# Norm sums and one row of b multiplied as rounded part plus rest in fp32r, and the first weight row issued from ScalarE's queue, in a two-layer decoder trunk on one core

## The chip, the core and the metric

The kernel runs on one core of one Trainium2 chip. The metric is device time in microseconds (us) of one execution; lower is better. Engines are named as the profile names them: PE (TensorE matmuls), PEld (its weight loads), DVE (VectorE), ACT (ScalarE), POOL (GpSimd) and SP (SyncE, which issues most DMAs).

## What is computed

One sequence of 256 tokens with 2048 channels goes through two layers. Layer 0 is a pooling mixer and a gated convolutional feed-forward network (FFN, width 5504); layer 1 is an attention with dilated windows and another such FFN. After each of the four parts comes a residual sum and a layer norm. All is float32.

```
for i in range(DEPTH):                      # DEPTH = 2
    mix = pool_mixer(h, ...) if i == 0 else dilated_attention(h, k_shared, v_shared, ...)
    h = layer_norm(ALPHA * h + mix, ln1_g[i], ln1_b[i])
    ff = conv_ffn(h, ffn_w_up[i], ffn_conv_w[i], ffn_conv_b[i], ffn_w_down[i])
    h = layer_norm(ALPHA * h + ff, ln2_g[i], ln2_b[i])

def layer_norm(x, g, b):
    mu = mean(x); var = mean((x - mu) ** 2)
    return (x - mu) * rsqrt(var + 1e-5) * g + b
```

## The kernel before

Activations lie channel-major: tile `H[q]` holds 4 blocks of 128 channels by 256 tokens. Every weight matrix is cut into units of 512 rows by up to 512 columns, over 360 of them, which run in one fixed list. `run_units` (the driver) takes them in order: it issues the loads of units up to `LD_AHEAD` = 5 ahead (`do_load`, L69, on SP's queue), splits the weights of units up to 3 ahead, runs the unit's matmuls on PE, and then runs small jobs that were put off with `later(n, fn)`.

The matrix products are made in fp32r, a rounded float32 format that PE multiplies in one pass. To keep precision each operand is split into a rounded part and the rest: `do_split` casts the weights on ACT (`wh`, L86) and subtracts on DVE (`wl`, L87). A product then takes three matmuls (L181 and L183, or L185 to L187).

Three of the four norms go through `chain`. By then DVE has summed the values and the squares of the 16 channel blocks into `ST["S"]` and `ST["Q"]`, 128x256 each. `chain` sums them over the 128 partitions with two plain fp32 matmuls against `invd`, a matrix of 1/2048 (L396, L397; the trace has two instructions for each). Then ACT squares the mean (L402), DVE subtracts (L403), ACT takes the root (L404), DVE the reciprocal (L405). The driver puts this job behind the last matmul of a unit; the split of the weights of three units on stands ahead of it on ACT and DVE.

The last norm works on tokens as rows. Once the first 128 tokens are complete `finish_first` normalises them (L729 on ACT; L686 times g and L735 plus b on DVE) while PE makes the rest of the last products. `finish_second` does the other 128 tokens with matmuls against diagonal matrices: L748, L753, L754 (`ident` times a row of b) and L758, and L762 on DVE makes the outputs, which L689 stores.

At the start SP issues the pieces of x and the rows of the first weight unit by turns; PE transposes x (L524); ACT, and for one half DVE, copies the result to `XC` (L530, L528), and the first products (L172) follow.

The order on every engine is that of the code: each engine takes its instructions in order. The pool `lnp` has one buffer for each tag, so a new tile of a tag waits until the last reader of the one before is done. The tag `fold2` is used by the folds, by `var` and by a small diagonal at the end; the tag `sq` by the squares, by `rm` and by `w3`.

Of the kernel before, what the change touches and what calls it, by code (L numbers as in the profile page):

```python
# [9 lines left out]
F32 = mybir.dt.float32  # L10
F32R = mybir.dt.float32r
I32 = mybir.dt.int32
AF = mybir.ActivationFunctionType
OP = mybir.AluOpType
# [3 lines left out]
T = 256  # L18
P = 128
# [14 lines left out]
def trunk(ctx: ExitStack, tc: tile.TileContext, x, pool_w_in, pool_w_grp, pool_scale, pool_w_out,  # L34
# [26 lines left out]
    def do_load(i, part=None):  # L61
        src = units[i][0]
        nk, n = src.shape[0] // P, src.shape[1]
        if not part:
            raw[i] = rawp.tile([P, nk, n], F32, name=f"raw{i}", tag="raw")
        rows = src.rearrange("(k p) n -> p k n", p=P)
        ks = pieces(i, nk)
        for s in ks if part is None else ks[2:] if part else ks[:2]:
            nc.sync.dma_start(raw[i][:, s], rows[:, s])  # L69

    parts = {}

# [201 lines left out]
    ident = const.tile([P, P], F32, name="ident")  # L274
    invd = const.tile([P, P], F32, name="invd")
    ones4 = const.tile([P, P], F32R, name="ones4")
    epst = const.tile([P, 1], F32, name="epst")
    inv = const.tile([P, 1, 16], F32, name="inv")
    cnt = const.tile([P, 3, P], F32, name="cnt")
# [113 lines left out]

    def chain(ps, lay, which, after):
        mean, msq = ps[:, :T], ps[:, T:]
        PE.matmul(mean, invd, ST["S"], start=True, stop=True)  # L396
        PE.matmul(msq, invd, ST["Q"], start=True, stop=True)  # L397
        t2 = lnp.tile([P, 2, T], F32, name="var", tag="fold2")
        rm = lnp.tile([P, 4, T], F32, name="rm", tag="sq")[:, 0:2]
        rs, mr = rm[:, 0:1, :], rm[:, 1:2, :]  # L400
        ST["rs"], ST["mr"] = rm[:, 0, :], rm[:, 1, :]
        A.activation(t2[:, 0, :], mean, AF.Square)  # L402
        V.tensor_tensor(t2[:, 1, :], msq, t2[:, 0, :], OP.subtract)  # L403
        A.activation(t2[:, 1, :], t2[:, 1, :], AF.Sqrt, bias=epst)  # L404
        V.reciprocal(rm[:, 0, :], t2[:, 1, :])  # L405
        V.tensor_tensor(rm[:, 1, :], mean, rm[:, 0, :], OP.mult)
        mb, rb = mr.to_broadcast([P, 4, T]), rs.to_broadcast([P, 4, T])
        g0 = 32 * which

        def spread():  # L410
            for i in range(4):
                PE.matmul(ps[:, i * P:i * P + P], one1, dg[:, i, :], start=True, stop=True)
            A.copy(rm.rearrange("p a t -> p (a t)"), ps)
            norm(0)

        def norm(q):
            V.tensor_tensor(H[q], H[q], rb, OP.mult)
            V.tensor_tensor(H[q], H[q], mb, OP.subtract)

        def affine(q):  # L420
            XC[q] = quad_tile("xc")
            for m in range(4):
                j = 4 * q + m
                A.activation(H[q][:, m, :], H[q][:, m, :], AF.Identity,
                             scale=vec[lay][:, g0 + j:g0 + j + 1], bias=vec[lay][:, g0 + 16 + j:g0 + 17 + j])
            A.copy(XC[q][:, :, 0, :T], H[q])

        def lo(q):
            lo_part(XC[q], H[q], 4)
            if after is not None:  # L430
                later((13, 16, 20, 22)[q], lambda: after(q))

        later(1, lambda: norm(0))
        for q in range(4):
            later(2 + q, lambda q=q: affine(q))
            if q < 3:
                later(2 + q, lambda q=q: norm(q + 1))
            later(3 + q, lambda q=q: lo(q))
# [75 lines left out]
    def x_quad(q, halves=(0, 1)):  # L514
        xin = XIN
        if halves[0] == 0:
            H[q] = hp.tile([P, 4, T], F32, name="h", tag="h")
            XC[q] = quad_tile("xc")
        for half in halves:
            ps = bank("xT")  # L520
            for kk in range(2):
                for t in range(2):
                    k = 2 * half + kk
                    PE.transpose(ps[:, kk * T + t * P:kk * T + t * P + P], xin[q, t][:, k * P:(k + 1) * P], ident)  # L524
            pv2 = ps.rearrange("p (k t) -> p k t", k=2)
            s = slice(2 * half, 2 * half + 2)
            if q == 0 and half == 1:
                V.tensor_copy(XC[q][:, s, 0, :T], pv2)  # L528
            else:
                A.copy(XC[q][:, s, 0, :T], pv2)  # L530
            V.tensor_tensor(XC[q][:, s, 1, :T], pv2, XC[q][:, s, 0, :T].bitcast(F32), OP.subtract)
            before.setdefault(min(q + 1, 3), []).append(lambda s=s, pv2=pv2: A.copy(H[q][:, s, :], pv2))
# [158 lines left out]
    def tm_post(c, first, last):  # L691
# [33 lines left out]
        def finish_first():  # L725
            rs, mr = scales(moments(0))
            for cc in range(4):
                z = HT[cc][:, 0, :]
                A.activation(z, z, AF.Identity, scale=rs, bias=mr)  # L729
            for cc in range(2):  # L730
                times_g(cc, 1)
            for cc in range(4):
                z = HT[cc][:, 0, :]
                times_g(cc, 0)
                V.tensor_tensor(z, z, ST["b"][:, cc, :], OP.add)  # L735
                store(cc, 0)

        def finish_second():
            def y(cc):
                return HT[cc][:, 1, :]  # L740

            def diag(nm, tag):
                return lnp.tile([P, P], F32, name=nm, tag=tag)

            g, b = ST["g"], ST["b"]
            w = [bank("w") for cc in range(3)]
            for cc in (0, 1):
                PE.matmul(w[cc], ident, y(cc), start=True, stop=False)  # L748
            mv = moments(1)
            dm, dn = diag("dm", "fold2"), diag("dn", "S")  # L750
            V.tensor_scalar(dm, ident, mv[:, 0:1], -1.0, op0=OP.mult, op1=OP.mult)
            for cc in (0, 1):
                PE.matmul(w[cc], dm, g[:, cc, :], start=False, stop=True)  # L753
            PE.matmul(w[2], ident, b[:, 2, :], start=True, stop=False)  # L754
            times_g(3, 1, slice(HC, 512))
            rs, mr = scales(mv)
            A.activation(dn, ident, AF.Copy, scale=mr)
            PE.matmul(w[2], dn, g[:, 2, :], start=False, stop=True)  # L758
            w3 = lnp.tile([P, 4, T], F32, name="w3", tag="sq").rearrange("p a t -> p (a t)")[:, :512]
            V.scalar_tensor_tensor(w3, g[:, 3, :], mr, b[:, 3, :], op0=OP.mult, op1=OP.add)  # L760
            for cc, u, v in ((0, w[0], b[:, 0, :]), (1, w[1], b[:, 1, :]), (3, y(3), w3), (2, y(2), w[2])):
                V.scalar_tensor_tensor(y(cc), u, rs, v, op0=OP.mult, op1=OP.add)  # L762
                store(cc, 1)
# [136 lines left out]
    with tc.tile_pool(name="start", bufs=1) as stp:  # L900
        for q in range(NQ):
# [12 lines left out]
            if q == 0:  # L914
# [4 lines left out]
                for i in range(WARM):  # L919
                    PE.matmul(warm[:, :P], invd, invd, start=True, stop=True)  # L920
        A.activation(ones4, invd, AF.Copy, scale=4.0)
        V.memset(epst, EPS)
        for c in range(16):
            nc.gpsimd.memset(inv[:, :, c:c + 1], 1.0 / (c + 1))
# [107 lines left out]
```

## Time and profile before

| | |
|---|---|
| median of 3 runs | 1926.71 us (1926.08 to 1928.01) |
| the profiled execution | 1925.69 us |
| its span, first to last instruction | 1923.9 us |
| PE busy | 1918.9 us, 11798 matmul instructions |
| DVE busy | 1413.9 us |
| ACT busy | 1010.7 us |
| DMA | 388.43 MB, mean 202 GB/s |

The profiled execution has 1.79 us outside its span. Busy times are those of single engines, which run side by side; matmuls are pipelined, so a busy PE need not be at its peak.

### The profile page before, as it was taken

The page shows a single profiled execution, that of the slowest core. Times are in us where ns is not written, and L with a number is a line of the kernel's source. Part 1 is how long each engine was busy: PE and PEld are TensorE (multiplying, and loading weights), DVE is VectorE, ACT ScalarE, POOL GpSimd, SP SyncE. Part 2 cuts the span into 40 slices and gives each one's busy share as a digit, 9 for nine tenths or more (in the row PEclk, how much of TensorE's full clock was granted, in tenths as well). Part 3 has the DMA queues.
Part 4 walks back from the last instruction along what each step waited for, and adds up shares of the span by engine and source line. Part 5 has one row for each costly group of instructions (what it writes and reads, how often), then busy time and mean ns, then how long its engine had stood idle before and what let it go on. Part 6 is the DMA issues. An engine that isn't in the chain of part 4 may idle for free.

```text
span 1923.9 us, 28630 instructions
## 1 busy us (share of the span) xinstructions
PE 1918.9 (100%) x11798; PEld 1758.9 (91%) x11798; DVE 1413.9 (73%) x1793; ACT 1010.7 (53%) x1106; POOL 102.5 (5%) x198
## 2 busy tenths in 40 slices
PE   9999999999999999999999999999999999999999
PEld 9999999999999999999999889999889988989997
DVE  7869888757766776789876767888756765775677
ACT  6545675445534535555644444576535543544552
POOL 2000000000000000000033210001320000000000
PEclk9999999999999999999999999999999999999999
DMA  8665556655565565556566655556875566555564
GB/s 281 227 204 196 175 194 222 219 197 198 197 210 204 182 214 193 195 182 219 171 218 213 197 170 190 189 190 209 244 225 196 199 202 211 199 197 200 183 213 148
DMA packets 200418, 388.43 MB, mean 202 GB/s; under 512 B 9582, under 2 KB 19972, under 8 KB 200032
## 3 DMA queue, kind: packets, MB, share of 16 engines
q1 hardware_dynamic: 194240, 381.71, 58.9%
q0 software_dynamic: 6048, 4.91, 1.2%
q8 instruction: 92, 1.51, 0.3%
q14 instruction: 38, 0.31, 0.0%
HBM read 380.01 MB, written 2.10 MB: 199 GB/s over the span
## 4 chain that ended last, share of the span: by engine, by line
PE 100%; DVE 0%; issue 0%
PE acc L181 48%; PE acc L183 24%; PE t L206 5%; PE t L207 5%; PE t L208 5%; PE acc L186 3%; PE acc L187 3%; PE acc L185 3%; PE acc L172 1%; PE s L823 0%; PE o L882 0%; PE xT L524 0%; PE s L822 0%; PE o L883 0%; PE warm L920 0%; PE w L753 0%
## 5 line engine op out<-in xcount | busy, mean ns | idle before, releaser
L87 DVE TENSOR_TENSOR wl<-raw,wh 128x2048 fp32r<-128x2048 f32 (+2 forms) x374 | 815.1, 2187 | 400.6 <-ACT wh L86 398.9
L181 PE MATMUL acc<-xc,wh 128*128 128x512 f32 x3072 | 1009.0, 382 | 0.0
L86 ACT CAST wh<-raw 128x2048 fp32r<-128x2048 f32 (+2 forms) x374 | 679.6, 1826 | 488.3 <-PE acc L181 276.0
L183 PE MATMUL acc<-xc,wl 128*128 128x256 f32 x3072 | 835.7, 272 | 0.0
L181 PEld LDWEIGHTS acc<-xc,wh 128*128 128x128 f32 x3072 | 577.6, 188 | 83.5 <-DVE o L885 0.5
L183 PEld LDWEIGHTS acc<-xc,wl 128*128 128x128 f32 x3072 | 589.8, 192 | 0.6 <-DVE wl L87 0.4
L181 PE MATMUL acc<-g,wh 128*128 128x512 f32 x644 | 211.2, 382 | 0.0
L183 PE MATMUL acc<-g,wl 128*128 128x256 f32 x644 | 175.2, 272 | 0.0
L593 DVE SCALAR_TENSOR_TENSOR c<-u,cv,c 128x256 f32<-128x256 f32 x344 | 141.8, 478 | 0.6
L181 PEld LDWEIGHTS acc<-g,wh 128*128 128x128 f32 x644 | 121.1, 188 | 17.6
L206 PE MATMUL t<-wh,g 128*128 128x512 f32 (+1 forms) x334 | 125.8, 377 | 0.0
L207 PE MATMUL t<-wl,g 128*128 128x512 f32 (+1 forms) x334 | 125.8, 377 | 0.0
L208 PE MATMUL t<-wh,g 128*128 128x512 f32 (+1 forms) x334 | 125.8, 377 | 0.0
L183 PEld LDWEIGHTS acc<-g,wl 128*128 128x128 f32 x644 | 123.6, 192 | 0.0
L185 PE MATMUL acc<-xp,wh 128*128 128x258 f32 x384 | 106.2, 276 | 0.0
L186 PE MATMUL acc<-xp,wh 128*128 128x258 f32 x384 | 105.7, 275 | 0.0
L187 PE MATMUL acc<-xp,wl 128*128 128x258 f32 x384 | 105.2, 274 | 0.0
L580 ACT COPY ut<-acc 128x256 f32<-128x256 f32 x156 | 56.4, 372 | 83.2 <-PE acc L183 83.2
L589 ACT ACTIVATE c<-u,cv 128x256 f32<-128x256 f32 x172 | 89.3, 591 | 0.4 <-DVE u L581 0.4
L181 PE MATMUL acc<-o,wh 128*128 128x512 f32 x256 | 84.5, 383 | 0.0
L181 PE MATMUL acc<-mixed,wh 128*128 128x512 f32 x256 | 84.0, 382 | 0.0
L186 PEld LDWEIGHTS acc<-xp,wh 128*128 128x128 f32 x384 | 73.3, 191 | 0.1
(215 smaller groups left out, 2050.1 us busy)
## 6 DMA issues: line engine op xcount, KB each, us to landing
raw<-in_ffn_w_up_dram SPq DMA_DIRECT2D x160, 1024.0 KB, 4.8
raw<-in_ffn_w_down_dram SPq DMA_DIRECT2D x80, 1024.0 KB, 5.1
raw<-in_pool_w_out_dram SPq DMA_DIRECT2D x16, 1024.0 KB, 5.1
raw<-in_shared_w_k_dram SPq DMA_DIRECT2D x16, 1024.0 KB, 5.1
raw<-in_attn_w_q_dram SPq DMA_DIRECT2D x16, 1024.0 KB, 5.8
raw<-in_shared_w_v_dram SPq DMA_DIRECT2D x16, 1024.0 KB, 5.6
raw<-in_attn_w_o_dram SPq DMA_DIRECT2D x16, 1024.0 KB, 5.1
raw<-in_pool_w_in_dram SPq DMA_DIRECT2D x12, 1024.0 KB, 6.7
```

Of the source, the lines that this page charges most:

```text
L86: A.copy(h, r)
L87: V.tensor_tensor(l, r, h.bitcast(F32), OP.subtract)
L181: PE.matmul(ps[m], h[:, k, c], q[:, k, :, :T].rearrange("p l (a c) -> p l c a", a=2), start=st, stop=False)
L183: PE.matmul(ps[m][:, :T], l[:, k, c], cols(k, 0), start=False, stop=sp)
L185: PE.matmul(ps[m][:, :n], h[:, k, c], cols(k, 0), start=st, stop=False)
L186: PE.matmul(ps[m][:, :n], h[:, k, c], cols(k, 1), start=False, stop=False)
L187: PE.matmul(ps[m][:, :n], l[:, k, c], cols(k, 0), start=False, stop=sp)
L206: PE.matmul(ps, xh, hk, start=first and k == 0, stop=False)
L207: PE.matmul(ps, xh, lk, start=False, stop=False)
L208: PE.matmul(ps, xl, hk, start=False, stop=last and k == nk - 1)
L589: A.activation(c[:, m, :], u[:, m, 2:], AF.Identity, scale=cv[:, 2, j:j + 1], bias=cv[:, 3, j:j + 1])
L593: V.scalar_tensor_tensor(c[:, m, :], u[:, m, i:i + T], cv[:, i, j:j + 1], c[:, m, :], op0=OP.mult, op1=OP.add)
```

## The change

1. In `chain` each sum is first split: ACT casts it to fp32r (`h[:, 0]`), DVE subtracts that from the sum (`h[:, 1]`), and PE makes two fp32r matmuls, one with each part. Both tiles `h` (named `sp`) have the tag `fold2`. Four fp32r matmuls stand in the place of two fp32 ones, three times in the program.
2. In the last norm one row group of b is split likewise into `b2`, in `finish_first`, and `finish_second` multiplies both parts with an fp32r identity instead of one fp32 product. `b2` takes the tag `sq`, and `w3` moves to another pool.
3. Row block 0 of the first weight unit is issued by ACT's queue instead of SP's, and the first half of x is cast on DVE instead of ACT.
4. `invr` and `identr`, fp32r copies of `invd` and `ident`, are made on DVE at the start.

```diff
@@ do_load
-            nc.sync.dma_start(raw[i][:, s], rows[:, s])
+            (nc.scalar if part == 0 and s.start == 0 else nc.sync).dma_start(raw[i][:, s], rows[:, s])
@@ chain
-        PE.matmul(mean, invd, ST["S"], start=True, stop=True)
-        PE.matmul(msq, invd, ST["Q"], start=True, stop=True)
+        for o, nm in ((mean, "S"), (msq, "Q")):
+            h = lnp.tile([P, 2, T], F32R, name="sp", tag="fold2")
+            A.copy(h[:, 0], ST[nm])
+            V.tensor_tensor(h[:, 1], ST[nm], h[:, 0].bitcast(F32), OP.subtract)
+            PE.matmul(o, invr, h[:, 0], start=True, stop=False)
+            PE.matmul(o, invr, h[:, 1], start=False, stop=True)
         t2 = lnp.tile([P, 2, T], F32, name="var", tag="fold2")
@@ x_quad
-            if q == 0 and half == 1:
+            if q == 0:
                 V.tensor_copy(XC[q][:, s, 0, :T], pv2)
@@ finish_first
             for cc in range(2):
                 times_g(cc, 1)
+            b2 = lnp.tile([P, 2, 512], F32R, name="b2", tag="sq")
+            A.copy(b2[:, 0], ST["b"][:, 2, :])
+            V.tensor_tensor(b2[:, 1], ST["b"][:, 2, :], b2[:, 0].bitcast(F32), OP.subtract)
+            ST["b2"] = b2
             for cc in range(4):
@@ finish_second
-            PE.matmul(w[2], ident, b[:, 2, :], start=True, stop=False)
+            for i in range(2):
+                PE.matmul(w[2], identr, ST["b2"][:, i], start=i == 0, stop=False)
-            w3 = lnp.tile([P, 4, T], F32, name="w3", tag="sq").rearrange("p a t -> p (a t)")[:, :512]
+            w3 = hp.tile([P, 4, T], F32, name="w3", tag="h").rearrange("p a t -> p (a t)")[:, :512]
@@ start
         A.activation(ones4, invd, AF.Copy, scale=4.0)
+        V.tensor_copy(invr, invd)
+        V.tensor_copy(identr, ident)
```

Where instructions now stand is shown at three places. The words in brackets name the semaphores that an instruction waits for: those that ACT (Activation), DVE, PE or a DMA queue (DMAHW, DMASW) raise.

The first place is the second of the three chains, after the FFN of layer 0. On DVE, before:

```order
L389 SCALAR_TENSOR_TENSOR xp<-h,vec_575,xp 128x2x128 [waits Activation_49] x4
L87 TENSOR_TENSOR wl_8347<-raw_8207,wh_8346 128x2048 [waits DMAHW1_49,Activation_49]
L87 TENSOR_TENSOR wl_8405<-raw_8271,wh_8404 128x2048 [waits DMAHW2_49,PE_49,Activation_49]
L87 TENSOR_TENSOR wl_8459<-raw_8344,wh_8458 128x2048 [waits DMAHW3_49,PE_49,Activation_49]
L403 TENSOR_TENSOR var<-acc,var 128x256 [waits Activation_49]
L405 RECIPROCAL rm<-var 128x256 [waits Activation_49]
```

And DVE after the change:

```order
L391 SCALAR_TENSOR_TENSOR xp<-h,vec_579,xp 128x2x128 [waits Activation_49] x4
L87 TENSOR_TENSOR wl_8359<-raw_8219,wh_8358 128x2048 [waits DMAHW1_49,Activation_49]
L87 TENSOR_TENSOR wl_8417<-raw_8283,wh_8416 128x2048 [waits DMAHW2_49,PE_49,Activation_49]
L87 TENSOR_TENSOR wl_8471<-raw_8356,wh_8470 128x2048 [waits DMAHW3_49,PE_49,Activation_49]
L401 TENSOR_TENSOR sp<-S,sp 128x256 [waits Activation_49]
L401 TENSOR_TENSOR sp<-Q,sp 128x256 [waits Activation_49]
L409 TENSOR_TENSOR var<-acc,var 128x256 [waits Activation_49]
L411 RECIPROCAL rm<-var 128x256 [waits Activation_49]
```

Both subtractions stand behind the three weight splits of later units (`wl`); before, nothing that PE needed for the sums stood there. On PE at the same place after the change, where before only L396 and L397 stood, each with a wait for DVE:

```order
L187 MATMUL acc<-xp,wl_8286 128x258
L402 MATMUL acc<-sp,invr 128x256 [waits Activation_49]
L403 MATMUL acc<-sp,invr 128x256 [waits DVE_49]
L402 MATMUL acc<-sp,invr 128x256 [waits Activation_49]
L403 MATMUL acc<-sp,invr 128x256 [waits DVE_49]
L185 MATMUL acc<-xp,wh_8358 128x258
```

Each of the four products now has a wait of its own, on ACT for a rounded part and on DVE for a rest, and the next unit's products stand behind them. ACT at the same place, after the change:

```order
L86 CAST wh_8416<-raw_8283 128x2048 [waits DMAHW2_49,PE_49]
L86 CAST wh_8470<-raw_8356 128x2048 [waits DMAHW3_49,PE_49,Activation_49]
L400 CAST sp<-S 128x256 [waits DVE_49]
L400 CAST sp<-Q 128x256 [waits PE_49]
L408 ACTIVATE var<-acc 128x256 [waits PE_49]
L410 ACTIVATE var<-var,epst 128x256 [waits DVE_49]
```

The cast of Q waits for PE: it writes the one `fold2` buffer, which PE's products of S read. Before, L402 (now L408) followed the weight casts directly.

The second place is `finish_first` on DVE, the first 128 tokens (`ht`), before:

```order
L722 SCALAR_TENSOR_TENSOR mv<-mv 128x1 [waits DVE_49]
L686 TENSOR_TENSOR ht<-ht,g 128x512 [waits DMAHW2_49]
L686 TENSOR_TENSOR ht<-ht,g 128x512
L686 TENSOR_TENSOR ht<-ht,g 128x512 [waits Activation_49]
L735 TENSOR_TENSOR ht<-ht,b 128x512 [waits DMAHW3_49,DVE_49]
```

And after the change:

```order
L692 TENSOR_TENSOR ht_12661<-ht_12661,g_17145 128x512 [waits DMAHW2_49]
L692 TENSOR_TENSOR ht_12870<-ht_12870,g_17145 128x512
L740 TENSOR_TENSOR b2_17225<-b_17163,b2_17225 128x512 [waits DMAHW3_49,Activation_49]
L692 TENSOR_TENSOR ht_12661<-ht_12661,g_17145 128x512
L745 TENSOR_TENSOR ht_12661<-ht_12661,b_17163 128x512 [waits DVE_49]
```

The subtraction for `b2` stands between the second and the third product with g, and waits for ACT's cast, which stands on ACT behind the four L729 (now L735) of this stage.

The third place is the start of ACT's program, before:

```order
L921 ACT_TABLE_LOAD
L921 ACTIVATE ones4_80<-invd_79 128x128 [waits DVE_49]
L530 CAST xc_151<-xT_152 128x2x256 [waits PE_49]
L86 CAST wh0_172<-raw0_92 128x512 [waits DMAHW2_49]
L86 CAST wh0_172<-raw0_92 128x512 [waits DMAHW3_49]
```

And after the change:

```order
L69 DMA raw0_94<-in_pool_w_in_dram 128x512
L932 ACT_TABLE_LOAD
L932 ACTIVATE ones4_80<-invd_79 128x128 [waits DVE_49]
L86 CAST wh0_176<-raw0_94 128x512 [waits DMAHW0_49]
L86 CAST wh0_176<-raw0_94 128x512 [waits DMAHW3_49]
```

The first weight row is issued ahead of everything else on ACT, and the cast of x, which stood ahead of the weight casts, has gone to DVE.

## Rows read from the trace of the kernel before

**Rows 1.** The page: chain of work that ended last, by engine.

```profile
PE 100%; DVE 0%; issue 0%
```

**Rows 2.** View of waits, engine PE: waiter, waited for, total us, times, longest us.

```profile
PE warm L920 <- DVE epst L922: 1.1, 1, 1.1
```

**Rows 3.** Timeline at the first chain: start us, duration us, engine, line, op.

```profile
208.08 4.49 DVE L87 TENSOR_TENSOR wl<-raw,wh 128x2048 fp32r<-128x2048 f32 x2
211.86 0.60 PE L396 MATMUL acc<-S,invd 128*128 128x256 f32 x2
212.93 0.38 ACT L402 ACTIVATE var<-acc 128x256 f32<-128x256 f32 x1 [3.54 <-PE acc L397]
213.34 0.42 DVE L403 TENSOR_TENSOR var<-acc,var 128x256 f32<-128x256 f32 x1 [0.78 <-ACT var L402]
```

**Rows 4.** Second chain: timeline; windows (stretch, length, busy PE to POOL, PEclk, DMA, GB/s).

```profile
892.74 6.68 DVE L87 TENSOR_TENSOR wl<-raw,wh 128x2048 fp32r<-128x2048 f32 x3
895.52 0.60 PE L396 MATMUL acc<-S,invd 128*128 128x256 f32 x2
896.49 0.28 PE L186 MATMUL acc<-xp,wh 128*128 128x258 f32 x1
896.58 0.38 ACT L402 ACTIVATE var<-acc 128x256 f32<-128x256 f32 x1 [0.75 <-PE acc L397]
899.34 0.41 DVE L403 TENSOR_TENSOR var<-acc,var 128x256 f32<-128x256 f32 x1
...
885.00:905.00 20.00, 20.00 (x178) 19.90 (x177) 19.22 (x23) 11.91 (x14) 0.00 (x0) 1.00 0.71 257
```

**Rows 5.** Timeline at the third chain.

```profile
1245.86 4.48 DVE L87 TENSOR_TENSOR wl<-raw,wh 128x2048 fp32r<-128x2048 f32 x2
1249.65 0.60 PE L396 MATMUL acc<-S,invd 128*128 128x256 f32 x2
```

**Rows 6.** Source and group views: duration ns min/median/max, first and last start (us); groups, mean ns.

```profile
L354 PEld LDWEIGHTS shift<-S,ones x3: 188/188/188, 148.5 to 1181.1; 128*128 128x128 f32 x3
L354 PE MATMUL shift<-S,ones x3: 286/286/286, 148.6 to 1181.2; 128*128 128x256 f32 x3
L356 ACT CAST cs<-shift x3: 372/373/377, 148.9 to 1181.5; 128x256 fp32r<-128x256 f32 x3
...
L885 DVE TENSOR_TENSOR o<-o 128x256 fp32r<-128x256 f32 x16 | 6.8, 425 | 14.0 <-ACT o L884 14.0
```

**Rows 7.** Timeline of the last 22 us.

```profile
1902.60 1.89 DVE L686 TENSOR_TENSOR ht<-ht,g 128x512 f32<-128x512 f32 x3
1902.72 2.93 ACT L729 ACTIVATE ht<-ht,mv 128x512 f32<-128x512 f32 x4 [0.43 <-DVE mv L722]
1914.58 0.42 DVE L698 TENSOR_TENSOR ht<-ht,t 128x256 f32<-128x256 f32 x1 [2.02 <-PE t L208]
1918.06 1.02 PE L754 MATMUL w<-b,ident 128*128 128x512 f32 x2
1918.92 1.02 PE L758 MATMUL w<-g,dn 128*128 128x512 f32 x2
1918.93 0.74 DVE L762 SCALAR_TENSOR_TENSOR ht<-ht,mv,w 128x512 f32<-128x512 f32 x1
1919.98 0.75 DVE L762 SCALAR_TENSOR_TENSOR ht<-ht,mv,w 128x512 f32<-128x512 f32 x1 [0.31 <-PE w L758]
```

**Rows 8.** Timeline of the start; SPq is SP's queue of DMA issues.

```profile
1.66 0.90 SPq L69 DMA_DIRECT2D raw<-in_pool_w_in_dram  x2
4.53 0.59 ACT L530 CAST xc<-xT 128x512 fp32r<-128x512 f32 x1 [2.19 <-PE xT L524]
5.69 1.63 PE L172 MATMUL acc<-xc,wh 128*128 128x256 f32 x8
8.65 1.30 ACT L86 CAST wh<-raw 128x512 fp32r<-128x512 f32 x2 [2.42 <-DMA raw<-in_pool_w_in_dram]
12.10 1.14 PE L172 MATMUL acc<-xc,wh 128*128 128x256 f32 x8
```

More of the change, by code (lines that the diff above doesn't have):

```diff
@@ L276, in trunk @@
     ones4 = const.tile([P, P], F32R, name="ones4")
+    invr = const.tile([P, P], F32R, name="invr")
+    identr = const.tile([P, P], F32R, name="identr")
     epst = const.tile([P, 1], F32, name="epst")
```

## The prediction, written before the changed kernel ran

> **What bounds the kernel now.** I read the chain of work that ended last first. It is PE for the whole span [rows 1], so a microsecond in which PE waits is a microsecond more, and work on ACT, DVE or DMA is free as long as PE doesn't wait for it. Then the waits: PE's own list holds one entry, 1.1 us before its first instruction [rows 2]. So PE can gain only where its own instructions get shorter, at the start, and in the tail after the last big product, where DVE has the lead. The timelines of those places come next, and the order of instructions beside them: what PE will wait for, and when the engine that makes it is free.
>
> **The three chains.** Removed are two fp32 products on PE each time. From L396's start to the first product behind them PE spends 0.86 us: at the second chain it starts at 895.52, and the second product behind it at 896.49, one product of 0.112 us (20 us hold 178 instructions) after the first at 896.38 [rows 4]. Added are four fp32r products of 0.112 us, 0.45 us together. If all operands lay ready each chain would gain 0.41 us, three of them 1.2 us. They don't lie ready; that is the main point.
>
> The rest of S is subtracted on DVE, behind the weight splits that stand ahead of it in DVE's order. When is DVE free? A split's record overlaps the next start by some 0.08 us: the three splits of the second chain end at 892.74 + 6.68 = 899.42, L403 starts at 899.34 [rows 4]. So the subtraction of S can start at 208.08 + 4.49 - 0.08 = 212.49 in the first chain [rows 3], at 899.34 in the second [rows 4] and at 1245.86 + 4.48 - 0.08 = 1250.26 in the third [rows 5]. PE arrives at 211.86, 895.52 and 1249.65 [rows 3 to 5]: 0.63, 3.82 and 0.61 us earlier. ACT is no obstacle in the first chain, where it waited 3.54 us for PE before L402 [rows 3]; in the second it is free at 896.58 - 0.75 = 895.83, 0.3 us after PE [rows 4], which DVE's delay covers.
>
> What follows is a round trip, for the two tiles `sp` share one buffer. The steps, from the time D at which DVE is free: the subtraction of S takes 0.42 us (L885, same shape) [rows 6]; 0.03 us of hand-over, as from L402's end at 213.31 to L403's start at 213.34 [rows 3]; a weight load ahead of the product, 0.1 us (148.5 to 148.6) [rows 6]. So the product with the rest of S starts at D + 0.55. ACT may overwrite the buffer 0.3 us after that start (148.6 to 148.9, the same product and a cast behind it) [rows 6]: D + 0.85. The cast of Q takes 0.37 us [rows 6], hand-over 0.03, subtraction 0.42, hand-over 0.03, weight load 0.1: the last product starts at D + 1.81, and the next unit's first product follows at D + 1.92. PE makes the product with the rounded part of Q within that time.
>
> - First chain: 212.49 + 1.92 = 214.41, against 211.86 + 0.86 = 212.72 before: +1.7 us.
> - Second: 899.34 + 1.92 = 901.26, against 896.38: +4.9 us.
> - Third: 1250.26 + 1.92 = 1252.18, against 1249.65 + 0.86 = 1250.51: +1.7 us.
>
> Together +8.3 us. The bounds: without hand-overs and without the weight loads (0.29 us a chain) 7.4 us; with 0.1 us more in each of the four hand-overs and in PE's end 9.8 us. If the second chain found DVE as late as the other two do (0.6 us), it would be +1.7 and the sum 5.1. I take 8.3, since every duration is that of the same shape. Queued behind the waiting cast on ACT and the waiting subtraction on DVE are L402 to L405 and the weight splits three units ahead; in the second chain L403 comes some 2.5 us later than before but PE 4.9 us later, and in the others both come 1.7 us later, so nothing new waits for them. That is why I add nothing for the norm behind the chain.
>
> **The tail.** One fp32 product of 512 columns goes: L754 holds PE from 1918.06 to 1918.92, 0.86 us [rows 7]. Two fp32r ones of twice 0.112 us each take 0.45 us, so PE is done 0.41 us earlier. DVE's last L762 waited only 0.31 us for PE, and its predecessor ran until 1919.67 [rows 7], so the gain is 0.31 us.
>
> Against it stands the split of b, which lies in DVE's queue between the second and the third L686, and waits for ACT's cast, which stands behind all four L729. Those end at 1902.72 + 2.93 = 1905.65 [rows 7]; a cast of 128x512 takes 0.65 us (two in 1.30) [rows 8]; 0.03 of hand-over; the subtraction 0.63 us (three L686 in 1.89) [rows 7]. So the third L686 starts at 1906.96 instead of 1902.60 + 1.26 = 1903.86, 3.1 us later. What hides this is DVE's wait before the last L698, 2.02 us [rows 7]; between the two DVE runs without a pause. 3.1 - 2.02 = 1.1 us come through to the norm of the last 128 tokens, which everything after it follows. The tail: +1.1 - 0.3 = +0.8 us (bounds: +0.5 if the cast is half as long and the hand-over nothing; +1.1 without the gain on PE).
>
> **The start.** SP needs 0.45 us to issue one weight row block (two in 0.90) [rows 8]; with the first on ACT's queue each later issue comes 0.45 us earlier. ACT cast x for 0.59 us from 4.53 and only then the first weight row, so the first product started at 5.69 [rows 8]. Now DVE casts x in 0.63 us (the pass of [rows 7]) while ACT casts the weights: the first product could start at 4.53 + 0.63 + 0.1 = 5.26, 0.43 us earlier. Half of that is lost, since PE is still slow there: eight products take 1.63 us from 5.69, and 1.14 us from 12.10 [rows 8]. Further on ACT waited 2.42 us for the third and fourth row blocks until 8.65 [rows 8], which a faster beginning doesn't hasten except by SP's earlier issues. And the row block now travels beside the first pieces of x. I take -0.2 us; bounds: -0.5 us (all of SP's issue time) and +0.4 us (x comes later than now).
>
> Here the Trainium skill has a rule, in "Trainium Kernel Development and Optimization", Key Constraints: DMAs from different issuing engines run on the same 16 DMA engines, and several issuers save only the sequencer's issue time. The 0.45 us of the row above is that time; by the rule no more than this can come back.
>
> The two copies for `invr` and `identr` run on DVE before it has anything else to do: ACT's cast of x waited 2.19 us for PE at 4.53 [rows 8], and DVE's first work followed that cast. Nothing for them.
>
> **The sum.** 8.3 + 0.8 - 0.2 = +8.9 us. The profiled execution, 1925.69 us with 1.79 us outside its span, would become 1934.6 us. The median of the runs is 1.0 us above it, so I predict 1926.71 + 8.9 = 1935.6 us.
>
> **The rivals.**
> - *PE's clock falls in the second chain.* PE would make one short product in the 0.7 us after its arrival, then nothing until 899.9, and three more products by 901.26: by far its longest pause. The granted clock reads 1.00 (2.4 GHz) through these 20 us [rows 4]. At the start, where PE began at 1.1 [rows 2], the eight products from 5.69 took 0.49 us more than those from 12.10 [rows 8]: some 4.4 of them ran at half rate, until 5.69 + 4.4 x 0.224 = 6.7. If the pause brings the clock down to 1.2 GHz and it stays so for 2 us up to the 5.6 us from 1.1 to 6.7, PE loses half of that, 1 to 2.8 us: 1936.6 to 1938.4 us. Against it: the pause is broken by products. The Trainium skill speaks for it: by "TensorE: Matmul & The Clock Gate", Part 1, the low clock is the default and activity releases it, so that a pause in mid-kernel can bring it back. No run here shows how long a pause it takes.
> - *The second chain is not late.* If the weight splits ahead of it end earlier than in this trace, PE waits 1.7 us there too: 1932.4 us. Against it: the three splits run without a gap, and ACT had cast for all of them by 895.83 [rows 4].
> - *Not slower: both splits are ready when PE arrives.* S and Q are complete before the weight splits begin. If the two subtractions ran there, PE would gain 0.41 us a chain, and with the tail's 0.31 and the start's 0.45 the time would be some 1924.7 us. The point of decision is DVE's free time against PE's arrival: it would have to be some 1.9 us earlier than PE, and is 0.6 to 3.8 us later in the rows. The order of instructions is fixed, so I see little for it.
> - *The rounded products are no shorter than the fp32 ones*, so that the change doesn't do what it says: then 0.41 us more a chain and in the tail, 1937 us. Against it speaks the 0.112 us a product of the second chain's stretch, which are fp32r.
>
> **How the numbers follow.** Forecast 0.52; clock falls 0.33; second chain not late 0.07; rounded products no shorter 0.02; not slower 0.03; the rest, 0.03, for something unseen at the start. Two tenths may be left out: the range goes from 1932.4, the second chain not late, to 1938.4, the top of the clock's case. A measurement of this kernel can tell about 0.2% from no change, 3.9 us: slower means above 1930.6, faster below 1922.9. Slower gathers the forecast, the clock, the late splits and the long products, 0.94 without a remainder for their errors; I say 0.93, the same 0.05, faster 0.02.
>
> **What would show it.** In the profile after: a new entry in PE's waits, for the subtraction `sp` on DVE, about 1.0, 3.4 and 1.0 us, then about 0.6 us for ACT's cast of Q and 0.2 us for the second subtraction each time; ACT's cast of Q waiting for PE; the first product behind each chain 2.6, 5.7 and 2.5 us after PE's arrival. In the tail no wait, or only a short one, before the last L698 (now L704), and a wait of DVE for ACT of some 2.4 us before `b2`. The first product at about 5.3 us. The clock's case would show PE's products at twice the duration behind the second chain. Wrong would make it: DVE taking the subtraction before the weight splits, or the two `sp` tiles not waiting for each other.

## The result, and the profile after

The changed kernel takes 1939.56 us (median of 6 runs, 1938.09 to 1940.83) against 1926.39 us (1925.79 to 1928.29) of the kernel before on the same chip: 13.2 us more, ratio 1.0068 [1.0058, 1.0078]. The forecast was 8.9 us more; the time lies 1.2 us above the range. The profiled execution took 1939.66 us, its span 1937.9 us: 14.0 us more than the 1923.9 us of before.

The page's chain of work, by engine, which was PE alone before [rows 1]:

```profile
PE 95%; DVE 4%; ACT 0%; issue 0%; DMA 0%; ACTq 0%; DVEq 0%
```

The view of waits, engine PE (waiter, waited for, total us, times, longest us):

```profile
PE acc L403 <- DVE sp L401: 4.8, 3, 3.2
PE acc L402 <- ACT sp L400: 2.0, 4, 0.5
PE warm L931 <- DVE invd L927: 1.1, 1, 1.1
PE w L763 <- DVE dm L761: 0.9, 1, 0.9
PE xT L530 <- DMA xin<-in_x_dram: 0.3, 1, 0.3
```

Before, one entry like the third was all that stood there [rows 2]. The two new ones for `sp` are the round trip of the prediction, 6.8 us; the fourth is the tail, the fifth the start. The four new waits come to 8.0 us, not to 14: the rest is not a wait. The timeline of the first chain, against [rows 3]:

```profile
212.10 0.28 PE L402 MATMUL acc<-sp,invr 128*128 128x256 f32 x1
212.72 0.41 DVE L401 TENSOR_TENSOR sp<-S,sp 128x256 fp32r<-128x256 f32 x1
213.19 0.38 PE L403 MATMUL acc<-sp,invr 128*128 128x256 f32 x1 [0.81 <-DVE sp L401]
213.61 0.40 ACT L400 CAST sp<-Q 128x256 fp32r<-128x256 f32 x1 [3.69 <-PE acc L403]
214.05 0.42 DVE L401 TENSOR_TENSOR sp<-Q,sp 128x256 fp32r<-128x256 f32 x1 [0.91 <-ACT sp L400]
214.07 0.38 PE L402 MATMUL acc<-sp,invr 128*128 128x256 f32 x1 [0.49 <-ACT sp L400]
214.53 0.38 PE L403 MATMUL acc<-sp,invr 128*128 128x256 f32 x1
214.75 0.27 PE L185 MATMUL acc<-xp,wh 128*128 128x258 f32 x1
214.86 0.28 PE L186 MATMUL acc<-xp,wh 128*128 128x258 f32 x1
...
215.09 0.43 PE L185 MATMUL acc<-xp,wh 128*128 128x258 f32 x1
215.31 0.42 PE L186 MATMUL acc<-xp,wh 128*128 128x258 f32 x1
```

Two things are to be seen here. PE goes through the chain as forecast: the first product behind it starts 2.65 us after PE's arrival at 212.10. But from 215.09 on the products start 0.22 us apart instead of 0.11. PE had been back at work for 0.3 us when it became slow. The lengths of the records, 0.42 instead of 0.28 us, show it less clearly than the distance of the starts. The second and third chain, against [rows 4, 5]:

```profile
899.87 0.39 PE L402 MATMUL acc<-sp,invr 128*128 128x256 f32 x1 [0.52 <-ACT sp L400]
903.48 0.39 PE L403 MATMUL acc<-sp,invr 128*128 128x256 f32 x1 [3.23 <-DVE sp L401]
904.36 0.44 PE L402 MATMUL acc<-sp,invr 128*128 128x256 f32 x1 [0.49 <-ACT sp L400]
905.20 0.42 PE L185 MATMUL acc<-xp,wh 128*128 128x258 f32 x1
905.42 0.42 PE L186 MATMUL acc<-xp,wh 128*128 128x258 f32 x1
...
1259.53 0.28 PE L402 MATMUL acc<-sp,invr 128*128 128x256 f32 x1
1262.17 0.27 PE L185 MATMUL acc<-xp,wh 128*128 128x258 f32 x1
...
1262.95 0.41 PE L186 MATMUL acc<-xp,wh 128*128 128x258 f32 x1
1263.16 0.42 PE L187 MATMUL acc<-xp,wl 128*128 128x258 f32 x1
```

In the third chain the slow products begin 0.8 us after PE has resumed (1262.95 against 1262.17); in the second they are slow when the chain ends.

The windows behind all three (stretch, length, busy PE to POOL with counts, PEclk, DMA, GB/s):

```profile
215.10:218.50 3.40, 3.40 (x18) 3.40 (x17) 2.52 (x4) 2.53 (x3) 0.00 (x0) 0.50 0.78 294
218.50:222.00 3.50, 3.50 (x34) 3.50 (x33) 3.47 (x4) 0.17 (x1) 0.00 (x0) 1.00 0.08 12
904.60:908.00 3.40, 3.38 (x16) 3.18 (x16) 1.74 (x3) 2.06 (x3) 0.00 (x0) 0.51 1.00 350
908.00:911.40 3.40, 3.40 (x32) 3.40 (x32) 3.37 (x4) 0.62 (x1) 0.00 (x0) 1.00 0.35 131
1263.00:1266.40 3.40, 3.40 (x19) 3.40 (x18) 2.79 (x4) 2.30 (x2) 0.00 (x0) 0.51 0.66 245
```

PE is busy in these stretches, yet makes 16 to 19 products where it makes 32 to 34 in the stretch that follows (32 behind the third chain too): the granted clock reads 0.50 or 0.51, so 1.2 GHz, behind each of the three chains. That is 13 to 16 products of 0.112 us fewer each time (the second stretch takes in the end of the chain itself). The busy share hides this (PE 99% on the page); the count of instructions and PEclk show it. It is no accident of one execution: the mean granted clock is 0.997 or 0.998 in all six runs of the changed kernel, and 1.000 in the profiled execution of the kernel before.

The start and the tail, against [rows 8] and [rows 7]:

```profile
3.83 1.31 PE L530 MATMUL xT<-ident,xin 128*128 128x128 f32 x4 [0.27 <-DMA xin<-in_x_dram]
6.08 1.50 PE L172 MATMUL acc<-xc,wh 128*128 128x256 f32 x8
...
1919.52 0.69 DVE L740 TENSOR_TENSOR b<-b,b 128x512 fp32r<-128x512 f32 x1 [2.31 <-ACT b L739]
1928.81 0.41 DVE L704 TENSOR_TENSOR ht<-ht,t 128x256 f32<-128x256 f32 x1
1930.47 1.98 PE L763 MATMUL w<-g,dm 128*128 128x512 f32 x4 [0.88 <-DVE dm L761]
```

The first product starts 0.39 us later than before, not earlier. In the tail DVE waits 2.31 us for the cast of b, its 2.02 us of wait before the last L704 are gone, and PE now waits 0.88 us for DVE.

**The account**, from the starts of the same products in both traces, as differences against the kernel before; "passing" is the time from PE's arrival at a chain to the first product behind it:

| part of the program | forecast, us | in the traces, us |
|---|---|---|
| start | -0.2 | +0.2 |
| passing the first chain | +1.7 | +1.8 |
| slow products behind it | 0 | +1.64 |
| passing the second chain | +4.9 | +5.2 |
| slow products behind it | 0 | +1.33 |
| between the second and the third chain | 0 | -0.3 |
| passing the third chain | +1.7 | +1.8 |
| slow products behind it | 0 | +1.64 |
| tail up to L763, and behind it | +1.1 and -0.3 | +0.9 and -0.4 |
| sum | +8.9 | +13.8 |

The spans differ by 14.0 us. (Second chain: the first product behind it starts at 905.20, at 896.38 before, so 8.82 later, of which 3.66 had come earlier; once the clock is back the products are 10.15 later.)

### The profile page after: what moved, and what is told of

It reads as the page before. It is cut to its first block, busy times and chain, and to the rows that moved or that the text cites. A ratio compares the mean times of both kernels' runs of the same rounds, so it can differ in the third digit from the quotient of the medians.

```text
span 1937.9 us, 28645 instructions
## 1 busy us (share of the span) xinstructions
PE 1924.5 (99%) x11798; PEld 1763.5 (91%) x11798; DVE 1418.9 (73%) x1803; ACT 1012.9 (52%) x1112; POOL 102.5 (5%) x198
## 4 chain that ended last, share of the span: by engine, by line
PE 95%; DVE 4%; ACT 0%; issue 0%; DMA 0%; ACTq 0%; DVEq 0%
PE acc L181 47%; PE acc L183 24%; PE t L208 5%; PE t L207 5%; PE t L206 5%; PE acc L187 2%; PE acc L185 2%; PE acc L186 2%; DVE wl L87 2%; PE acc L172 1%; DVE xp L391 0%; PE s L834 0%; PE o L893 0%; DVE fold L337 0%; DVE h L310 0%
```

## The experiments

Two theories. A: each pause brings PE's clock down by itself, and this low clock is what the sum lacks. B: the missing 4.6 us are something else, such as a norm behind the chain that comes late, and the low clock is a mark of it or of the rounded products. Times are compared with runs of the kernel before on the same chip.

**e1_fill.** The changed kernel with products that serve nothing (8 ahead of the split products of each sum, 37 for S in the second chain) filling PE's waits.

```diff
...
+            for i in range(37 if nm == "S" and ST["n"] == 2 else 8):
+                PE.matmul(msq, invr, XP[0][:, 0, 0, :T], start=True, stop=True)
```

> The changed kernel with PE kept at work while it waits in the three chains: 8, 37 and 8 extra fp32r products of 256 columns before the product with the rounded part of S, and 8 each time before that of Q. They write the half of the PSUM bank that Q's product overwrites, so the result is the same; the waits for DVE and ACT stay as they are. Theory A (the pauses take PE's clock down to 1.2 GHz behind each chain, 1.7 + 1.4 + 1.7 = 4.8 us of the loss): no stretch of half granted clock, PE leaves each chain as late as in the changed kernel (2.5, 5.8 and 2.5 us after its arrival), and the time is 1939.6 - 4.8 = 1934.8 us, within 1 us. Theory B (the products behind the chains are slow because ACT and DVE are late with the weight splits, or because of the DMAs running there): nothing is regained, 1939.6 us or more.

Measured: 1936.13 us against 1925.86, ratio 1.0052 [1.0036, 1.0069]. The span is 1934.1 us, 3.8 less than without fillers. Windows behind the first and second chain:

```profile
215.50:219.00 3.50, 3.50 (x32) 3.50 (x32) 2.11 (x2) 2.61 (x3) 0.00 (x0) 1.00 0.95 353
904.40:908.00 3.60, 3.60 (x34) 3.60 (x34) 2.39 (x3) 2.68 (x3) 0.00 (x0) 1.00 1.00 362
```

No low clock, in all four runs (mean granted clock 1.000), although PE passes the first and third chain in about the same time as in the changed kernel (1.8 and 1.7 us more than before). In the trace the products behind the three chains lose nothing, against 4.6 us in the changed kernel. The rounded products, the late DVE and ACT and the busy DMAs (shares of 0.95 and 1.00) are all still there, so none of them makes the products slow: this speaks for A. The time alone does so less well. The median is 1.3 us above A's number, and over the kernel before only 2.9 us of the 4.6 came back; in the profiled execution (1935.87 us) 0.9 us more than in the changed kernel's went at the start, where PE's products became fast later (below), and some 0.8 us stay open.

**e10_fill_1_3.** The same fillers in the first and third chain alone; the edit against e1_fill:

```diff
-            for i in range(37 if nm == "S" and ST["n"] == 2 else 8):
+            for i in range(0 if ST["n"] == 2 else 8):
```

> The changed kernel with filler products in the waits of the first and third chain alone, none in the second. Theory A (each pause brings TensorE's clock down by itself, and fillers take each fall away by themselves): half clock only behind the second chain, 1.7 us less for each of the other two than in the changed kernel: 1936.2 us. Theory B (the clock is not set by the pauses, or the loss is not the clock's): 1939.6 us as without fillers, with low clock behind the first and third chain too.

Measured: 1938.2 us (1937.38 to 1938.82) against 1926.2, ratio 1.0062 [1.0048, 1.0076]: between the numbers of the two theories, so the time alone decides nothing. The windows do:

```profile
215.10:218.50 3.40, 3.40 (x33) 3.40 (x33) 2.47 (x3) 2.59 (x3) 0.00 (x0) 1.00 0.81 302
...
904.60:908.00 3.40, 3.40 (x18) 3.40 (x18) 2.79 (x4) 2.30 (x2) 0.00 (x0) 0.52 0.72 266
...
1263.00:1266.40 3.40, 3.40 (x33) 3.40 (x32) 3.32 (x3) 1.80 (x2) 0.00 (x0) 1.00 0.41 151
```

Only the unfilled second chain has the low clock, and the traces show 1.6 us saved behind each of the other two. In the second chain the clock fell earlier here, within the wait: the product with the rest of S at 901.93 already took 0.58 us, 0.39 in the changed kernel, and chain and clock cost 0.8 us more. So at which point of a pause the clock falls is not the same in each trace. (The profiled execution is the fastest of the four.)

**e2_two_buffers.** One tile for all four parts in another pool, so that the cast of Q no longer waits for PE's products of S.

```diff
...
-            h = lnp.tile([P, 2, T], F32R, name="sp", tag="fold2")
+        if "sp" not in ST:
+            ST["sp"] = hp.tile([P, 2, 2, T], F32R, name="sp", tag="h")
...
+            h = ST["sp"][:, i]
```

> The changed kernel with the splits of S and Q in separate buffers, so that ACT's cast of Q no longer waits for PE's products of S. DVE's place for the subtractions stays behind the weight splits. By the steps of the forecast the last product of a chain follows DVE's release by 0.42 + 0.42 + 0.03 + 0.1 us instead of 1.81, so each chain is 0.84 us shorter, 2.5 us together. Theory A: if the clock still falls behind all three chains, 1937.1 us; if the shorter pauses of the first and third chain (1.7 us) no longer bring it down, 3.4 us less, 1933.7 us; the granted clock shows which. Theory B: 1937.1 us whatever the clock does.

Measured: 1933.67 us against 1925.86, ratio 1.0041 [1.0026, 1.0056]: 7.8 us more than the kernel before, where the change takes 13.2 more. The wait for ACT stands in PE's waits once now, for the second chain; the windows are those behind the first and the second chain:

```profile
PE acc L405 <- DVE sp L403: 4.9, 3, 3.2
PE acc L404 <- ACT sp L402: 0.5, 1, 0.5
```

```profile
214.00:217.00 3.00, 3.00 (x28) 3.00 (x28) 1.79 (x2) 2.29 (x3) 0.00 (x0) 1.00 1.05 396
901.80:905.20 3.40, 3.40 (x18) 3.40 (x17) 2.27 (x3) 2.68 (x3) 0.00 (x0) 0.50 1.01 342
```

PE passes the first chain in 1.65 us (212.37 to 214.02), where the changed kernel took 2.65, the third likewise, and the clock stays at 1.00 behind both. So the shared buffer cost twice: some 1.0 us a chain by itself, and 1.6 us behind the first and the third, where the clock fell only with the longer pauses. These two lengths are all that the runs show; where between them the fall begins, and whether it hangs on the length alone, was not measured.

**e3_fp32_sums.** Start and tail as changed, the sums in fp32 as before.

```diff
...
-            PE.matmul(o, invr, h[:, 0], start=True, stop=False)
-            PE.matmul(o, invr, h[:, 1], start=False, stop=True)
+        PE.matmul(mean, invd, ST["S"], start=True, stop=True)
+        PE.matmul(msq, invd, ST["Q"], start=True, stop=True)
```

> The changed kernel with the sums of the chains multiplied in fp32 again, as before the change; the tail with b2 and the start as changed. If the chains are the loss, 1926.4 + 0.2 (start) + 0.4 (tail) = 1927.0 us, and no stretch of half clock. If tail or start carry more than their timelines show, over 1928 us.

Measured: 1927.21 us against 1925.86, ratio 1.0007 [0.9998, 1.0016]: 1.35 us, an amount whose interval still holds no change at all, so the chains make up nearly all of the 13.2. **e5_start_only** and **e6_tail_only** part the rest further: the kernel before with the start alone changed, or the tail alone. Of the two edits:

```diff
+            (nc.scalar if part == 0 and s.start == 0 else nc.sync).dma_start(raw[i][:, s], rows[:, s])
+            if q == 0:
                 V.tensor_copy(XC[q][:, s, 0, :T], pv2)
...
+            for i in range(2):
+                PE.matmul(w[2], identr, ST["b2"][:, i], start=i == 0, stop=False)
```

> The kernel before with the start alone changed: the first weight row issued by ACT's queue, the first half of x cast on DVE. The forecast had -0.2 us for it. Theory now (the row travels beside the first pieces of x, so x lands later and the first product with it): PE's first transposition at 3.8 to 4.0 us instead of 3.35, the first product at about 6.1 instead of 5.7, the time 0.3 to 0.6 us longer, 1926.3 us against 1925.9. Rival (SP's earlier issues come back): first product at 5.3, 1925.6 us. The times may not tell these apart, the timeline of the start does.

> The kernel before with the split of b alone (b2 in finish_first, two fp32r products, w3 in another pool). By the forecast's steps DVE starts the rest of finish_first 3.1 us later, its wait before the last L698 (2.0 us) goes, 1.1 us come through, 0.3 to 0.4 us come back from PE: the diagonal's product 1.0 us later, the end 0.7 us later, 1926.6 us against 1925.9. Rival (the delay is absorbed, since DVE's rows run closer than read): the end 0.3 us earlier, 1925.6 us.

Measured: 1926.79 us, ratio 1.0002 [0.9993, 1.0011], and 1927.2 us, ratio 1.0005 [0.9996, 1.0014], against 1926.21. Neither can be told from no change by time; the rows tell the mechanism. The start in e5:

```profile
0.74 0.41 ACTq L69 DMA_DIRECT2D raw<-in_pool_w_in_dram  x1
3.87 1.32 PE L524 MATMUL xT<-ident,xin 128*128 128x128 f32 x4 [0.31 <-DMA xin<-in_x_dram]
6.12 1.31 PE L172 MATMUL acc<-xc,wh 128*128 128x256 f32 x8
```

The row goes out at once, but the transposes now wait for x, whose first piece lands at 3.73 us instead of 3.10, and the first products start at 6.12 instead of 5.69. In e6 the split of b waits 2.31 us for ACT as in the changed kernel, and the last L699 no longer waits:

```profile
1915.99 0.41 DVE L699 TENSOR_TENSOR ht<-ht,t 128x256 f32<-128x256 f32 x1
```

**e4_early_split.** The rival "both splits are ready when PE arrives", made to happen: cast and subtraction follow the last folds, ahead of the weight splits, in a buffer of their own.

```diff
                 xp(3, lay, which)
...
+                for i, nm in enumerate("SQ"):
+                    h = ST["sp"][:, i]
+                    A.copy(h[:, 0], ST[nm])
+                    V.tensor_tensor(h[:, 1], ST[nm], h[:, 0].bitcast(F32), OP.subtract)
                 later(2 if first else 3, lambda: chain(ps[0], lay, which, after))
```

> The changed kernel with the splits of S and Q made as soon as the sums are complete, ahead of the weight splits in the order of ACT and DVE, in a buffer of their own; PE's four products stay where they are. The operands then lie ready some 2 us before PE arrives, PE has no pause and the clock stays up: 3 x 0.41 us less than with fp32 sums, 1927.0 - 1.2 = 1925.8 us. Rival: the weight splits, now 0.85 us later on DVE, are late for PE instead; then PE waits for wl behind the chains and the time is 1927 to 1929 us.

Measured: 1926.62 us against 1925.86, ratio 1.0003 [0.9994, 1.0013]. Some 12 us of the change's 13 are gone, so the place of the split was the loss, together with the shared buffer, which this edit removes too (e2_two_buffers prices it). The 0.8 us above the forecast hold a new wait of PE in the second chain, 0.9 us for `rm`, which e7 shows as well. **e7_best** also takes the start back and puts the split of b behind the first half of the third column group, where DVE and ACT wait anyway.

```diff
...
-            b2 = lnp.tile([P, 2, 512], F32R, name="b2", tag="sq")
+            if t == 0 and c == 2:
+                ST["b2"] = b2 = lnp.tile([P, 2, 512], F32R, name="b2", tag="sq")
```

> The splits of S and Q made early on DVE as in e4, the split of b made while DVE waits for the last products (behind the first half of column group 2), the start as before the change. First and third chain 0.41 us shorter each; in the second DVE's weight splits and the steps behind them come 0.85 us later and the next unit waits 0.9 us for rm, which e4 showed: +0.5 us there; the tail 0.3 us shorter. Together -0.6 us, 1925.3 us against 1925.9. If the weight splits are late elsewhere, no gain.

Measured: 1925.58 us, ratio 0.9995 [0.9986, 1.0004]. PE passes the first chain as the rival said:

```profile
211.82 0.28 PE L405 MATMUL acc<-sp,invr 128*128 128x256 f32 x1
...
212.29 0.27 PE L185 MATMUL acc<-xp,wh 128*128 128x258 f32 x1
```

0.47 us instead of 0.86, in the first and third chain. In the second more than the gain is given back: PE goes in 0.4 us ahead of the kernel before and ends 0.4 us behind it. PE's waits have the entry:

```profile
PE acc L185 <- DVE rm L415: 0.9, 1, 0.9
```

The two subtractions put DVE's later steps off by some 0.8 us against PE's products there, and the next group's product has to wait until `rm` has read its bank. **e8_best_pool** moves the subtractions to POOL; the edit against e7_best:

```diff
-                    V.tensor_tensor(h[:, 1], ST[nm], h[:, 0].bitcast(F32), OP.subtract)
+                    nc.gpsimd.tensor_tensor(h[:, 1], ST[nm], h[:, 0].bitcast(F32), OP.subtract)
```

> As e7, but the two subtractions of each chain on POOL, which has nothing to do there, so DVE's order is that of the kernel before. If POOL makes each within 1.5 us, the rests are ready when PE arrives and no wait for rm is left: 3 x 0.41 + 0.3 = 1.5 us less than before, 1924.4 us against 1925.9. Rival: POOL is slower than that, or takes DVE's time while it runs; then PE waits in the chains, and a pause there over some 2 us brings the clock down, 1927 us or more.

Measured: 1926.23 us, ratio 1.0002 [0.9993, 1.0011]. DVE was relieved of 0.8 us and lost more: its four L397 took 2.62 us beside POOL's two subtractions, 1.66 us in e7_best, and as much at the other two chains. (The "some 2 us" of the expectation lies between the two pauses measured, 1.65 and 2.65 us; no run placed it.)

```profile
891.18 2.62 DVE L397 SCALAR_TENSOR_TENSOR xp<-h,vec,xp 128x256 fp32r<-128x256 f32 x4
...
890.83 1.02 POOL L332 TENSOR_TENSOR sp<-S,sp 128x256 fp32r<-128x256 f32 x1 [518.64 <-ACT sp L331]
891.83 0.90 POOL L332 TENSOR_TENSOR sp<-Q,sp 128x256 fp32r<-128x256 f32 x1
```

**e9_two_chains.** e7 with the second chain left in fp32.

```diff
...
+                for i, nm in enumerate("SQ" if first else ""):
...
+        if not first:
+            PE.matmul(mean, invd, ST["S"], start=True, stop=True)
+            PE.matmul(msq, invd, ST["Q"], start=True, stop=True)
```

> The split copies and rounded products in the first and third chain alone, with the subtraction made early on VectorE, the second chain in fp32 as before, and the output group's split moved behind the first half of the next column group. If VectorE's late steps in the second chain are what ate the gain of the version with all three chains, the two chains give 0.4 to 0.5 us each and the tail 0.3: 1.1 to 1.3 us less than the kernel before, ratio 0.9994, and no product waits for a step of VectorE behind the second chain. Rival: the gain of the chains is lost in the rest of the program, as the waits of other engines set the pace there; then ratio 1.0000 to 0.9998.

Measured: 1925.92 us against 1926.2, ratio 0.9999 [0.999, 1.0008]. The wait for `rm` is gone and PE's last products start 0.98 us earlier than before, but the span is 0.2 us longer. The view of DMA from 1919 us on (a slice is 0.14 us):

```profile
GB/s 387 194 283 343 402 357 387 417 358 387 343 402 417 358 402 402 328 105 75 0 0 0 0 15 0 0 0 0 0 0 0 0 0 0 0 0 0 0 0 0
...
q14 instruction: 1, 0.01, 0.7%
```

The last store is all but through at 1921.6; a rest of it moves 0.6 us later, and one packet of the instruction queue lies in this stretch, where the kernel before has none. That packet lasts from 1921.56 to 1922.18, and the last packet of the store with data begins at 1922.18. **e11_pad** adds two one-column copies each on ACT and DVE ahead of the tail, which serve nothing, to shift that load; **e12_chains_only** is e9 with b in fp32. The edits, against e9:

```diff
+                for i in range(2):
+                    A.copy(lnp.tile([P, 1], F32, name="padA", tag="pre"), epst)
+                    V.tensor_copy(lnp.tile([P, 1], F32, name="padV", tag="pre"), epst)
```

```diff
...
-            for i in range(2):
-                PE.matmul(w[2], identr, ST["b2"][:, i], start=i == 0, stop=False)
+            PE.matmul(w[2], ident, b[:, 2, :], start=True, stop=False)
```

> The version with the first and third chain split early and the output group's split, and beside that split two more copies of one column each on ScalarE and on VectorE. Its predecessor had PE's products 0.98 us earlier than the kernel before at the end and yet a span 0.2 us longer; an 8-KB packet of the instruction queue lay at 1921.6 to 1922.2, between the last packets of the last store. Theory: that load of instructions held up the last store; with some more instructions on the way it lies earlier, as it does in the version with three chains (1910.9), and the gain arrives: span 1923.0, 0.9 us under the kernel before, ratio 0.9995. Rival: the end was late for another reason or by chance; then the span stays at about 1924 and the ratio at 0.9999.

> The split and rounded products in the first and third chain alone, with the early subtraction; b of the last group stays fp32, the start as before. Two chains give 0.2 us of product time and 0.2 us behind it each, 0.6 us in all as the trace of the version with the output group's split shows up to the last column groups (-0.59): span 1923.3, ratio 0.9997, if no load of instructions falls beside the last store; 1924 if one does.

Measured: 1924.94 us, ratio 0.9994 [0.9986, 1.0003], and 1924.99 us, ratio 0.9995 [0.9986, 1.0004], against 1926.13. In e11 the stretch has no packet of the instruction queue and the store ends in one piece:

```profile
GB/s 432 313 164 328 402 343 387 402 343 417 357 372 417 343 417 372 387 343 45 0 0 0 0 0 0 0 0 0 0 0 0 0 0 0 0 0 0 0 0 0
```

Its span is 1923.2 us, 0.9 less than e9's with four instructions more. That the load of instructions held up the store agrees with both traces, and with the medians; it is one place in one kernel, and nothing but the shift by e11 tests it. e12's profiled execution waited 1.6 us for its first weights and is no witness. The medians of these two versions are 1.2 us under the kernel before, but both intervals hold 1, so the runs do not show a gain.

## Why the prediction was wrong

The step that failed is the price of the low clock, which the sum put at nothing. The fall of PE's clock was held possible in the second chain alone, as a rival with 0.33, because that pause was "by far its longest". It fell behind all three. In these traces the first and third chain, with 2.65 us from PE's arrival to the first product behind them and four short products in that time, were enough; the same two at 1.65 us were not (e2_two_buffers). This is 1.64 + 1.33 + 1.64 = 4.6 us that the sum lacks; filling the pauses takes the low clock away (e1_fill), and chain by chain (e10_fill_1_3). So theory B has fallen. That the top of the range, 1938.4 us, comes near the measured time is luck: it pays 2.8 us for one fall, where there were three of 1.3 to 1.6 us.

- **The chains' passing**: +1.8, +5.2, +1.8, forecast +1.7, +4.9, +1.7: right, step by step. The list of PE's waits was forecast as 1.0, 3.4, 1.0 for the rest of S and 0.6 for the cast of Q, and shows 0.81, 3.23, 0.81 and 0.49. The 0.2 for the rest of Q does not show as a wait. The fourth wait for ACT is for the cast of S in the second chain, 0.52 us, which I had covered by DVE's delay, and it is covered.
- **The clock's price**: the rival put 1 to 2.8 us on one fall, the lower end from a stay of 2 us for which it has no row; rows show 1.3 to 1.6. Its sign, products at twice the duration, shows in the starts, 0.22 instead of 0.11 us apart, not in the lengths of the records. The rule that I cited from the Trainium skill, "TensorE: Matmul & The Clock Gate", Part 1 (low clock is the default, activity releases it), agrees with the windows above: PEclk 0.50, then 1.00 again after more products. I weighed it for one pause only, although the forecast itself had the same row of waits three times. What I took as evidence against it, "the pause is broken by products", is what the runs refuted.
- **The tail**: +0.5 net, forecast +0.8: right in mechanism. The wait of 2.31 us on b and the vanished 2.02 us are as forecast; PE's shorter products gave 0.4, not 0.3.
- **The start**: forecast -0.2, measured +0.2 in the profile (first product +0.39). The bound of +0.4 held, the value had the wrong sign: x comes later beside the row block, and all that ACT's freedom gave is lost. By the Trainium skill, "Trainium Kernel Development and Optimization", Key Constraints, a second issuer saves issue time alone, and e5 agrees: SP's next pieces of x went out at 2.12 us instead of 2.60, but the first piece landed later, not earlier.
- **The rival "both splits ready"**: its price of 0.41 us a chain holds in e7 (0.39), and its condition, DVE before PE, is what the loss hung on: e4, which makes it true by the order of instructions and a buffer of its own, takes some 12 of the 13 us away. No version came out clearly faster than the kernel before.

## What to carry to other kernels

A cheaper product on the engine that bounds gains only if its operands are ready before that engine arrives: put the preparing steps where their input appears, ahead of the long jobs in the same queue, and look at who is pushed back by them. Count a pause of PE as more than its length: test each pause, short products in it or not, for a half-clock stretch behind it, by the count of products in equal windows. A tag that two tiles share in one chain turns two waits into a round trip.

## What was not expected of the hardware

- PE's clock fell 0.3 us after PE had resumed (215.09 against 214.75) and in the third chain 0.8 us after (1262.95 against 1262.17), as well as inside a pause (e10, where the product at 901.93 was slow), so the wait itself can look clean.
- At the start the moment at which PE's products become fast differs from trace to trace with the same instructions there: in e1_fill the eight first products took 2.05 us, in the changed kernel 1.50 (1.63 before [rows 8]). In e1_fill 0.9 us of the first chain's lateness come from there, so a difference of 1 us between two executions says little. The row of e1_fill:

```profile
6.26 2.05 PE L172 MATMUL acc<-xc,wh 128*128 128x256 f32 x8
```

- POOL's subtraction of 128x256 took 0.90 to 1.02 us, DVE's 0.42, and while POOL ran four DVE operations took 2.62 instead of 1.66 us.
- A load of instructions of 8 KB can lie beside the last store: the span of e11 is 0.9 us shorter than that of e9 with four one-column copies more and no such load there. That the load was the cause rests on this pair of traces.
